# Two more output tiles between the last products of a projection, and a gate tile in front of a moment

## The chip, the cores and the metric

One NeuronCore of one Trainium2 chip runs the whole program. TensorE (PE in the profile, its weight loads PEld) multiplies 128 by 128 weight blocks with 128 x n operands and sums into banks of PSUM; VectorE (DVE), ScalarE (ACT) and GpSimd (POOL) do the rest; SyncE (SP) issues most of the DMAs. The metric is the device time of the program in microseconds, less is better.

## The reference

One inference step of a backbone of two layers over 640 tokens (512 latent and 128 context tokens) of width 1024: layer 0 mixes tokens by attention, layer 1 by a linear recurrence; each is followed by a SwiGLU feed-forward, and each sub-layer adds its output, times a gate, to the residual stream after a modulated RMS norm. The change lies where layer 1's recurrence ends and its feed-forward begins:

```python
y = (hs_f + hs_b).astype(xm.dtype) * jax.nn.gelu(gate)
return y @ w_out, ...                       # the recurrent output's projection
...
lat = lat + g1_l[:, None, :] * o_l          # residual, the same for ctx
f_l = _swiglu(_modulate(lat, norm_g[i, 1], sh2_l, sc2_l), ffn_w_gu[i], ffn_w_down[i])
```

with

```python
def _rms_norm(x, g):
    xf = x.astype(jnp.float32)
    y = xf * lax.rsqrt(jnp.mean(xf * xf, axis=-1, keepdims=True) + RMS_EPS)
def _swiglu(x, w_gu, w_down):
    gate, up = jnp.split(x @ w_gu, 2, axis=-1)
    return (jax.nn.silu(gate) * up) @ w_down
```

## The kernel before

**Layout.** Features lie on partitions, tokens along the free dimension. A width of 1024 is KT = 8 blocks of 128, and the 640 tokens are two halves CH of HT = 320. A float32 product is made of three: every operand is split into a high part (rounded to fp32r) and a low part (what is left), and a tile, one block of 128 outputs over one half of the tokens, sums high x high, high x low and low x high over the eight input blocks k: 24 matmuls. `chunk` and `some` (L235 to L237) write this for the projections, `plain` (L1189 to L1191) for the first feed-forward tiles.

**Weights.** `unit` loads a weight block (L169) into one of three `raw` buffers, makes its high part with ScalarE (L182, a cast) or, with `cast=True`, by a second load from DRAM on POOL's DMA queue that casts on the way (L180), and its low part with VectorE (L184). Slot "m" uses `whi`, `wlo`, slot "x" `whx`, `wlx`, three buffers each; the first `whx` of every three has a place of its own. `after` names an instruction of VectorE behind which the low part is put.

**Order.** The program is traced in the order of the code; a scheduler of the framework then sets the order of each engine's instructions by its own estimate of when each is ready, the earlier in the code first. An engine runs them in that order. `pin` (`issue_after`) is the only thing by which the code sets an order: the instructions in it come behind a named one of the same engine.

**PSUM.** Eight banks: one `at` for the sums of squares, three `mm`, three `mx`, one `mc`. `ps(tag)` takes a bank of a tag. `pg()` counts its calls and gives `mx` where the count modulo 5 is 1 or 3, else `mm`; `pg(False)` counts too, and always gives `mm`. The spread of a moment has no tag of its own in this phase and takes `mx`.

**`project_halves` (L1043).** It multiplies the recurrence's output y by its projection. Output blocks are f = 0 to 7. Five tiles begin early (both halves of 0 and 1, the first half of 2) with the input blocks k that are there; `turn` (L1054) then adds the last blocks k = 5, 6, 7 to all of them as VectorE delivers y (L1058 with y's high part, L1060 with its low part). y's last block comes in two halves of tokens, so `turn(KT - 1, ...)` is done for the tiles of the first half and then for those of the second. Block 3's first half stands between and around these (L1075): its weights' low part is pinned behind `ended`, VectorE's last step of the recurrence, and the last third of its products comes after the second `turn`. Blocks 4 to 7, first half, follow, then the first half's statistics, and then blocks 2 to 7 of the second half.

Each finished tile goes through `out`: VectorE adds it to x times the gate (L605), `square` makes ScalarE square the new x (L539, L542) and VectorE add the square to `ssq` (L544, block 7 excepted, whose square the matmuls take themselves), and SP stores x (L1046). `stat` is `moment` and `spread`: TensorE sums `ssq` over partitions (L558, L561), VectorE makes the variance (L563), POOL the power -1/2 (L565), VectorE a diagonal (L567), and TensorE spreads it over the partitions (L575). ScalarE copies the result (L1089), and `normed` (L1009 on VectorE, L1010 on ScalarE) and `halve` (L1422, L1424) make the normalised tokens and their high and low parts, the blocks B11 and B21 of the first half (`first_half`), B12 and B22 of the second (`second_half`).

**The feed-forward.** Of its 22 pairs of gate and up blocks, the first three (PLAIN) are six ordinary tiles for each half of the tokens: gate, up, gate, up, gate, up. `ffn_halves` loads all six weights, the low parts of the second and third pair pinned behind the last `ssq` addition (`self.sq`), and calls `plain` for the first half. `held` (L1122) keeps the second tile, the first up, behind the moment (at k = 0), and its blocks from k = 5 and the later tiles behind the spread, so that its first five blocks lie over the chain between the two. The gate tiles end in a Silu (L1197), the up tiles in a product (L1151). Then the second half's tokens are normalised, `plain` runs for them, `sums` and `sum_weights` form differences of tokens and of weights (POOL, L1033 and L1110) for the other 19 pairs, which use a scheme of seven products in place of eight, and the projection down is woven in between.

Of the kernel before, what the change touches and what calls it, by code (L numbers as in the profile page):

```python
# [12 lines left out]
ALU = mybir.AluOpType  # L13
# [4 lines left out]
KT = D // P  # L18
# [4 lines left out]
CH = ((0, 320), (320, 640))  # L23
# [6 lines left out]
NF = FF // P  # L30
# [12 lines left out]
HT = NTOK // 2  # L43
HB = KH * HT
DEH = 6
PLAIN = 3
# [77 lines left out]
def _pieces(t0, t1):  # L124
    return [(s, max(a, t0), min(b, t1)) for s, a, b in ((0, 0, NLAT), (1, NLAT, NTOK)) if max(a, t0) < min(b, t1)]


class _Step:
# [473 lines left out]
    def residual(self, f, t0, t1, ps, G, sq):  # L602
        for s, a, b in _pieces(t0, t1):
            xs = self.x[:, f, a:b]
            self.nc.vector.scalar_tensor_tensor(xs, ps[:, a - t0:b - t0], G[:, s, f:f + 1], xs, ALU.mult, ALU.add)  # L605
        if sq:
            self.square(f, t0, t1)

# [431 lines left out]
        self.halve("T4", k, self.x[:, k + KH, 0:HT])  # L1040
        self.nc.sync.dma_start(self.x[:, k + KH], xd[(k + KH) * P:(k + KH) * P + P])

    def project_halves(self, w, hi, lo, gk, key, xd, ended):  # L1043
        def out(f, t0, t1, ps):
            self.residual(f, t0, t1, ps, G, True)
            self.nc.sync.dma_start(xd[f * P:f * P + P, t0:t1], self.x[:, f, t0:t1])  # L1046
        G = self.need(self.gcols, gk)
        us = [self.unit(w[f], "mmx"[f], cast=f == 2) for f in range(3)]
        early = [(f, t0, t1) for f in range(3) for c, (t0, t1) in enumerate(CH) if c == 0 or f < KT - DEH]
        pss = [(self.ps("mx") if j % 2 else self.pg(False))[:, 0:HT] for j in range(len(early))]  # L1050
        for (f, t0, t1), ps in zip(early, pss):
            self.some(us[f], hi, lo, t0, t1, ps, range(KT - 3))

        def turn(k, turns, pin=None):  # L1054
            for (f, t0, t1), ps in turns:
                for part in us[f]:
                    with self.pin(pin):
                        pin = self.done = self.nc.tensor.matmul(ps, part[:, k], hi[:, k, t0:t1], start=False, stop=False).ins  # L1058
            for (f, t0, t1), ps in turns:
                self.done = self.nc.tensor.matmul(ps, us[f][0][:, k], lo[:, k, t0:t1], start=False, stop=(k == KT - 1)).ins  # L1060
                if k == KT - 1:
                    with self.pin(self.low):
                        out(f, t0, t1, ps)
        sides = [[e for e in zip(early, pss) if e[0][1:] == c] for c in CH]
        for k in range(KT - 3, KT - 1):
            turn(k, sides[0] + sides[1])
        us.append(self.unit(w[3], "m", ended, cast=True))
        turn(KT - 1, sides[0])
        t0, t1 = CH[0]
        ps = self.ps("mx")[:, 0:HT]  # L1070
        for j, (part, v) in enumerate(((0, hi), (0, lo), (1, hi))):
            if j == 2:
                turn(KT - 1, sides[1], self.done)
            for k in range(KT):
                self.done = self.nc.tensor.matmul(ps, us[3][part][:, k], v[:, k, t0:t1], start=(j == k == 0),  # L1075
                                                  stop=(j == 2 and k == KT - 1)).ins
        out(3, t0, t1, ps)
        for f in range(4, KT):
            us.append(self.unit(w[f], "xm"[f % 2]))
            out(f, *CH[0], self.chunk(us[f], hi, lo, *CH[0], pins={0: self.done} if f == 4 else {}))  # L1080
        self.rt = self.t([P, NTOK], F32, "r", 2)
        for c, (t0, t1) in enumerate(CH):
            for f in range(KT - DEH, KT) if c else ():
                out(f, t0, t1, self.chunk(us[f], hi, lo, t0, t1))
                j = f - KT + DEH
                for k in range(max(0, 2 * j - 2), 2 * j) if f < KT - 1 else ():
                    self.first_half(k, key)
            self.stat(t0, t1)
            self.nc.scalar.copy(self.rt[:, t0:t1], self.r[0][:, 0:t1 - t0])  # L1089

    def gate_weights(self, l, f):
# [89 lines left out]
    def plain(self, us, c, xd=None):  # L1181
        nc, n = self.nc, 0
        for j, pair in enumerate(us):
            for u, (hi, lo) in enumerate(pair):
                ps = self.pg()[:, 0:HT]
                for k in range(KT):
                    xh, xl = [self.X[f"B{1 + k // KH}{1 + c}{p}"][:, k % KH] for p in "hl"]
                    with self.held(n, k):
                        nc.tensor.matmul(ps, hi[:, k], xh, start=(k == 0), stop=False)  # L1189
                    nc.tensor.matmul(ps, hi[:, k], xl, start=False, stop=False)  # L1190
                    nc.tensor.matmul(ps, lo[:, k], xh, start=False, stop=(k == KT - 1))  # L1191
                n += 1
                if u:
                    self.hidden(j, c, ps, g)
                else:
                    g = self.t([P, HT], F32, "g", 3, self.sb)
                    nc.scalar.activation(g, ps, AF.Silu)  # L1197
            if c:
                self.sums(j, xd)

    def ffn_halves(self, l, key, xd):
        us = [[self.unit(self.i["gu"][l, c * NF + f], None, self.sq if f else None) for c in range(2)] for f in range(PLAIN)]
        self.hold = True
        self.plain(us, 0)
        self.hold = False
        self.wx, self.share = 0, False
        qs = [None] * PLAIN
        for k in range(KH):
            self.second_half(k, key)
        self.plain(us, 1, xd)  # L1210
        for k in range(KH - 1):
            self.last_sum(k, xd)

        def rest():
            self.sums(KH - 1, xd)
            self.last_sum(KH - 1, xd)
        f0 = 0
        for ci, n in enumerate(CHN):
            for j in range(n):
                f = f0 + j  # L1220
                if f < PLAIN:
                    continue
                if f == len(qs):
                    qs.append(self.gate_weights(l, f))
                    self.pair_a(qs[f])
                if j:
                    self.sum_weights(qs[f])
                    self.pair_c(qs[f - 1])
                    self.last_weights(qs[f])
                self.pair_b(qs[f], j)  # L1230
            if f >= PLAIN:
                self.pair_c(qs[f])
            w = self.i["dn"][l, :, :, f0:f0 + n]
            f0 += n
            if f0 == NF:
                self.share = True
                self.project_last(w, self.hhi, self.hlo, (l, 5))
            else:
                qs.append(self.gate_weights(l, f0))
                self.pair_a(qs[f0])  # L1240
                self.sum_weights(qs[f0])
                self.last_weights(qs[f0])
                self.project_part(w, self.hhi, self.hlo, (l, 5), rest if f0 == PLAIN else None)
# [57 lines left out]
    def turn(self, table, step):  # L1301
        if table != self.table:
            self.table = table
            with self.pin(self.last_act):
                self.last_act = self.nc.scalar.preload_act_table(table).ins
        with self.pin(self.last_act):
            self.last_act = step().ins
# [139 lines left out]
    def run(self):  # L1447
        nc, tc, i, o = self.nc, self.tc, self.i, self.o
# [68 lines left out]
        xd = dram.tile([D, NTOK], F32, tag="xd", name="xd")  # L1517
# [11 lines left out]
        yhi = self.big()  # L1529
        ylo = self.big()  # L1530
        wp = self.ctx.enter_context(tc.tile_pool(name="wp", bufs=1, reuse_waits="tile"))
        with self.phase("lru", at=1) as lp:
            A, B, C, G = {}, {}, {}, {}
# [14 lines left out]
            for t in range(KT + 2):  # L1548
# [7 lines left out]
                if t > KT:  # L1556
                    ended = self.lru_end(t - 2, *B.pop(t - 2), G.pop(t - 2), yhi, ylo)
# [11 lines left out]
        with self.phase("ffn1", at=1, mx=3, mc=1, wx=2) as fp:  # L1569
            self.X = {}  # L1570
            self.blocks(x1, ("B11h", "B11l", "B21h", "B21l"))
            self.blocks(x2, ("B22h", "B22l", "T1h", "T1l"))
            self.blocks(self.t([P, 2 * KH, HT], F32R, "xt", 1, fp), ("T4h", "T4l"))
            self.X["B12h"], self.X["B12l"] = self.X["T4h"], self.X["T4l"]
            self.project_halves(i["wlo"], yhi, ylo, (1, 2), (1, 1), xd, ended)
            nc.gpsimd.dma_start(o["nh"], self.st)
            self.hhi, self.hlo = self.big(n=PITCH), self.big(n=PITCH)
            for t, n in ((self.hhi, "T2"), (self.hlo, "T3")):
                self.blocks(t, (n + "h", n + "l"))
            self.hhi, self.hlo = [t[:, :, 0:NTOK] for t in (self.hhi, self.hlo)]  # L1580
            self.ffn_halves(1, (1, 1), xd)
# [19 lines left out]
```

## Time and profile before

| | us |
|---|---|
| median of 3 runs | 1512.21 (1511.01 to 1512.85) |
| profiled execution | 1510.6 |
| its span, first to last instruction | 1508.8 |
| TensorE busy | 1482.4 |
| VectorE busy | 1061.8 |
| ScalarE busy | 698.1 |
| `project_halves` on TensorE, from about | 985 to 1063 |

A row of the timeline has a start, a duration, engine, line, operation, output and inputs, the count, and in brackets the idle time of the engine just before it with what ended it. A row of a window has its stretch and length, busy time and instructions of PE, PEld, DVE, ACT and POOL, the granted TensorE clock (1.00 is full), the DMA engines' busy share and GB/s. The waits list engine, line, what it waited for, total, times and the longest. Matmuls overlap: one of 320 columns is shown as 0.31 us long, while the next starts 0.15 us after it.

### The profile page before, as it was taken

To read this page: it belongs to the slowest core of one execution; us is meant where nothing else is said; L and a number is where in the kernel's file an instruction comes from. 1 tells how busy PE (TensorE), PEld (TensorE's weight loads), DVE (VectorE), ACT (ScalarE), POOL (GpSimd) and SP (SyncE) were. 2 spreads that over 40 slices of the span, in tenths; PEclk is the share of its full clock that TensorE was granted. 3 is DMA by queue.
4 is the path that set the end of the run, shared out by engine and by line. 5 is a ranking of instruction groups with operands and counts; after the bars stand their busy time and mean duration, and the time that the engine had idled before them with its cause. 6 is when DMAs were issued, how large, how long until landed. Compare 5 with 4: busy or idle time off the path is not lost. (4 is left out here: it accounts for less than half of the span.)

```text
span 1508.8 us, 26147 instructions
## 1 busy us (share of the span) xinstructions
PE 1482.4 (98%) x10389; PEld 1434.3 (95%) x10389; DVE 1061.8 (70%) x2017; ACT 698.1 (46%) x1267; POOL 229.3 (15%) x264
## 2 busy tenths in 40 slices
PE   9999999999999999999999999999999999999997
PEld 6999999899999999999999988889999999999997
DVE  5778998679989997434443768986875665665555
ACT  4676766664332123312321569875534342524243
POOL 0112232101111110000000000000431323232211
PEclk9999999999999999999999999999999999999999
DMA  9655765446556664222222444334243131313221
GB/s 376 175 145 159 189 187 172 118 152 184 184 179 205 203 201 141 62 85 84 65 76 84 156 135 123 119 127 171 77 134 95 59 113 56 112 57 101 67 57 70
DMA packets 72905, 198.34 MB, mean 131 GB/s; under 512 B 8112, under 2 KB 24656, under 8 KB 72656
## 3 DMA queue, kind: packets, MB, share of 16 engines
q1 hardware_dynamic: 57392, 142.32, 29.8%
q0 software_dynamic: 14816, 53.69, 11.9%
q8 instruction: 81, 1.33, 0.4%
q10 hardware_dynamic: 576, 0.68, 0.1%
q14 instruction: 40, 0.33, 0.1%
HBM read 180.53 MB, written 8.92 MB: 126 GB/s over the span
## 5 line engine op out<-in xcount | busy, mean ns | idle before, releaser
L236 PE MATMUL mm<-big,whi 128*128 128x320 f32 (+3 forms) x1215 | 377.6, 311 | 1.0 <-DVE big L1424 0.7
L235 PE MATMUL mm<-big,whi 128*128 128x320 f32 (+3 forms) x1215 | 375.6, 311 | 2.9 <-DVE x L605 1.4
L237 PE MATMUL mm<-big,wlo 128*128 128x320 f32 (+3 forms) x1215 | 375.2, 310 | 0.0
L235 PEld LDWEIGHTS mm<-big,whi 128*128 128x128 f32 x1215 | 228.0, 188 | 5.3 <-issue 1.6
L236 PEld LDWEIGHTS mm<-big,whi 128*128 128x128 f32 x1215 | 228.4, 188 | 3.1 <-DVE big L1424 1.3
L237 PEld LDWEIGHTS mm<-big,wlo 128*128 128x128 f32 x1215 | 228.7, 188 | 1.1
L264 DVE SCALAR_TENSOR_TENSOR mprod<-mraw,csb 128x1024 f32<-128x1024 f32 x160 | 195.1, 1219 | 12.1 <-DMA mraw<-in_wm 11.6
L605 DVE SCALAR_TENSOR_TENSOR x<-mm,G,x 128x128 f32<-128x128 f32 (+2 forms) x193 | 77.8, 434 | 78.1 <-PE mm L237 78.1
L182 ACT CAST whi<-raw 128x1024 fp32r<-128x1024 f32 (+1 forms) x70 | 72.8, 1040 | 112.4 <-PE mm L236 64.3
L184 DVE TENSOR_TENSOR wlo<-raw,whi 128x1024 fp32r<-128x1024 f32 (+1 forms) x87 | 105.7, 1215 | 22.9 <-ACT whi L182 10.1
L236 PE MATMUL mm<-big,whx 128*128 128x320 f32 (+3 forms) x357 | 110.9, 311 | 0.0
L237 PE MATMUL mm<-big,wlx 128*128 128x320 f32 (+3 forms) x357 | 110.5, 310 | 0.0
L235 PE MATMUL mm<-big,whx 128*128 128x320 f32 (+3 forms) x357 | 110.2, 309 | 0.0
L260 POOL DMA_DIRECT2D mraw<-in_wm x80 | 42.9, 537 | 352.7 <-DVE mprod L264 254.0
L236 PE MATMUL mx<-big,whi 128*128 128x320 f32 (+3 forms) x285 | 88.1, 309 | 0.0
L235 PE MATMUL mx<-big,whi 128*128 128x320 f32 (+3 forms) x285 | 88.0, 309 | 0.0
L237 PE MATMUL mx<-big,wlo 128*128 128x320 f32 (+3 forms) x285 | 87.9, 308 | 0.0
L182 ACT CAST whx<-raw 128x1024 fp32r<-128x1024 f32 (+1 forms) x39 | 40.1, 1028 | 85.8 <-PE mm L236 48.2
L236 PE MATMUL mx<-big,whx 128*128 128x320 f32 (+3 forms) x248 | 76.8, 310 | 0.0
L237 PE MATMUL mx<-big,wlx 128*128 128x320 f32 (+3 forms) x248 | 76.8, 310 | 0.0
L235 PE MATMUL mx<-big,whx 128*128 128x320 f32 (+3 forms) x248 | 76.5, 308 | 0.0
L1422 ACT CAST whi<-raw 128x1024 fp32r<-128x1024 f32 (+1 forms) x41 | 41.3, 1007 | 72.0 <-PE mm L236 44.5
(388 smaller groups left out, 3721.3 us busy)
## 6 DMA issues: line engine op xcount, KB each, us to landing
raw<-in_gu SPq DMA_DIRECT2D x88, 512.0 KB, 3.5
mraw<-in_wm POOLq DMA_DIRECT2D x80, 512.0 KB, 4.0
raw<-in_dn SPq DMA_DIRECT2D x24, 512.0 KB, 3.7
sw<-in_wm SPq DMA_DIRECT2D x16, 512.0 KB, 10.9
raw<-in_wqk SPq DMA_DIRECT2D x16, 512.0 KB, 4.8
raw<-in_wi SPq DMA_DIRECT2D x16, 512.0 KB, 3.5
whi<-in_wi POOLq DMA_DIRECT2D x16, 512.0 KB, 3.8
raw<-in_dn SPq DMA_DIRECT2D x16, 448.0 KB, 3.3
```

The costliest lines, as they stand in the source:

```text
L182: nc.scalar.copy(hi, raw)
L184: self.low = nc.vector.tensor_tensor(lo, raw, hi.bitcast(F32), ALU.subtract).ins
L235: nc.tensor.matmul(ps, hi[:, k], xhi[:, k, s], start=(k == 0), stop=False)
L236: nc.tensor.matmul(ps, hi[:, k], xlo[:, k, s], start=False, stop=False)
L237: self.done = nc.tensor.matmul(ps, lo[:, k], xhi[:, k, s], start=False, stop=(k == last)).ins
L260: nc.gpsimd.dma_start(w, self.i["wm"][l * 6 + j - 2, f])
L264: nc.vector.scalar_tensor_tensor(prod, w, 1.0, self.csb[:, s], ALU.mult, ALU.mult, accum_out=out[:, s, f:f + 1])
L605: self.nc.vector.scalar_tensor_tensor(xs, ps[:, a - t0:b - t0], G[:, s, f:f + 1], xs, ALU.mult, ALU.add)
L1422: self.nc.scalar.copy(hi, v)
```

## The change

`project_halves`: blocks 3 and 4 are both loaded before the last `turn`s, both with `cast=True`, block 4's low part pinned behind block 3's. The first half of block 4 gets the bank `mc`. Their products are chained by pins in a fixed order: first `turn`, two thirds of block 3, second `turn`, two thirds of block 4, the last third of 3, the last third of 4. Block 5's low part is pinned behind the residual of block 2's first half, and its first half takes an `mm` bank by name; 6 and 7 go on with `pg()`.

`ffn_open` starts the generator into which `plain` is turned. It is called when the last tile of the second half is out: the first pair's weights are loaded (the up's low part now also pinned behind `self.sq`), the first gate tile is traced, then the moment, then the first five blocks of the up tile, then the spread, pinned behind those. The rest follows as before.

```diff
@@ residual
-            self.nc.vector.scalar_tensor_tensor(xs, ...)
+            self.added = self.nc.vector.scalar_tensor_tensor(xs, ...).ins
@@ project_halves
-        us.append(self.unit(w[3], "m", ended, cast=True))
+        for f in (3, 4):
+            us.append(self.unit(w[f], "xm"[f % 2], ended, cast=True))
+            ended = self.low
+        t0, t1 = CH[0]
+        more = {f: self.ps(v)[:, 0:HT] for f, v in ((3, "mx"), (4, "mc"))}
+
+        def part(f, pieces):
+            for p, v in pieces:
+                for k in range(KT):
+                    with self.pin(self.done):
+                        self.done = self.nc.tensor.matmul(more[f], us[f][p][:, k], v[:, k, t0:t1], start=(v is hi and p == k == 0),
+                                                          stop=(p == 1 and k == KT - 1)).ins
         turn(KT - 1, sides[0])
-        t0, t1 = CH[0]
-        ps = self.ps("mx")[:, 0:HT]
-        for j, (part, v) in enumerate(((0, hi), (0, lo), (1, hi))):
-            if j == 2:
-                turn(KT - 1, sides[1], self.done)
-            for k in range(KT):
-                self.done = self.nc.tensor.matmul(ps, us[3][part][:, k], v[:, k, t0:t1], start=(j == k == 0),
-                                                  stop=(j == 2 and k == KT - 1)).ins
-        out(3, t0, t1, ps)
-        for f in range(4, KT):
+        added = self.added
+        part(3, ((0, hi), (0, lo)))
+        turn(KT - 1, sides[1], self.done)
+        part(4, ((0, hi), (0, lo)))
+        for f in (3, 4):
+            part(f, ((1, hi),))
+            out(f, t0, t1, more[f])
+        us.append(self.unit(w[5], "m", added))
+        more[5] = self.pg(False)[:, 0:HT]
+        part(5, ((0, hi), (0, lo), (1, hi)))
+        out(5, t0, t1, more[5])
+        for f in range(6, KT):
             us.append(self.unit(w[f], "xm"[f % 2]))
-            out(f, *CH[0], self.chunk(us[f], hi, lo, *CH[0], pins={0: self.done} if f == 4 else {}))
+            out(f, t0, t1, self.chunk(us[f], hi, lo, t0, t1))
...
-            self.stat(t0, t1)
+            if c:
+                first = opening()
+                next(first)
+                moment = self.moment(t0, t1)
+                next(first)
+                with self.pin(self.done):
+                    self.spread(moment)
+            else:
+                self.stat(t0, t1)
@@ plain
+                    if self.hold and n == 1 and k == 5:
+                        yield
                     with self.held(n, k):
-                        nc.tensor.matmul(ps, hi[:, k], xh, start=(k == 0), stop=False)
+                        self.done = nc.tensor.matmul(ps, hi[:, k], xh, start=(k == 0), stop=False).ins
...
+                yield
@@ ffn_open, ffn_halves
+    def ffn_open(self, l):
+        self.us = [[self.unit(self.i["gu"][l, c * NF], None, self.sq if c else None) for c in range(2)]]
+        self.first = self.plain(self.us, 0)
+        self.hold = True
+        return self.first
+
     def ffn_halves(self, l, key, xd):
-        us = [[self.unit(self.i["gu"][l, c * NF + f], None, self.sq if f else None) for c in range(2)] for f in range(PLAIN)]
-        self.hold = True
-        self.plain(us, 0)
+        us, gu = self.us, self.i["gu"]
+        us += [[self.unit(gu[l, c * NF + f], None, self.sq) for c in range(2)] for f in range(1, PLAIN)]
+        for _ in self.first:
+            pass
```

More of the change, by code (lines that the diff above doesn't have):

```diff
@@ L604, in residual @@
             xs = self.x[:, f, a:b]
-            self.nc.vector.scalar_tensor_tensor(xs, ps[:, a - t0:b - t0], G[:, s, f:f + 1], xs, ALU.mult, ALU.add)
+            self.added = self.nc.vector.scalar_tensor_tensor(xs, ps[:, a - t0:b - t0], G[:, s, f:f + 1], xs, ALU.mult, ALU.add).ins
         if sq:
@@ L1041, in last_sum, with project_halves @@
         self.nc.sync.dma_start(self.x[:, k + KH], xd[(k + KH) * P:(k + KH) * P + P])
-    def project_halves(self, w, hi, lo, gk, key, xd, ended):
+    def project_halves(self, w, hi, lo, gk, key, xd, ended, opening):
         def out(f, t0, t1, ps):
@@ L1209, in ffn_halves @@
             self.second_half(k, key)
-        self.plain(us, 1, xd)
+        for _ in self.plain(us, 1, xd):
+            pass
         for k in range(KH - 1):
@@ L1574, in run @@
             self.X["B12h"], self.X["B12l"] = self.X["T4h"], self.X["T4l"]
-            self.project_halves(i["wlo"], yhi, ylo, (1, 2), (1, 1), xd, ended)
+            self.project_halves(i["wlo"], yhi, ylo, (1, 2), (1, 1), xd, ended, lambda: self.ffn_open(1))
             nc.gpsimd.dma_start(o["nh"], self.st)
```

## The prediction, made before the changed kernel was run

> **Names.** f3a is output tile 3 over tokens 0 to 319, f3b over tokens 320 to 639, so too for f0 to f7. g0, u0, g1, u1, g2, u2 are the six feed-forward tiles over the first tokens in program order; u0 is the one that L1188 holds behind the moment and the spread. A tile is 24 matmuls.
>
> **What bounds the kernel now.** I read the page first, then TensorE's waits, then its stretches by window around L1043.
>
> ```profile
> span 1508.8 us, 26147 instructions
> PE 1482.4 (98%) x10389; PEld 1434.3 (95%) x10389; DVE 1061.8 (70%) x2017; ACT 698.1 (46%) x1267; POOL 229.3 (15%) x264
> ```
>
> ```profile
> PE at L558 <- DVE ssq L544: 4.5, 2, 3.8
> ```
>
> ```profile
> 1006.20:1015.40 9.20, 6.47 (x41) 5.65 (x40) 8.50 (x17) 3.02 (x5) 0.55 (x1) 1.00 0.40 143
> 1015.40:1052.60 37.20, 37.18 (x258) 37.12 (x258) 23.18 (x49) 17.90 (x35) 0.87 (x1) 1.00 0.56 197
> 1052.60:1056.60 4.00, 0.19 (x2) 0.03 (x1) 3.32 (x9) 2.96 (x7) 0.00 (x0) 1.00 0.22 82
> 1057.60:1061.00 3.40, 3.40 (x16) 3.40 (x15) 2.37 (x4) 0.00 (x0) 0.85 (x1) 0.50 0.69 205
> ```
>
> TensorE is busy 98% of the span, so only its holes are worth anything, and the longest in the whole trace, 3.8 us, is the one before the last moment (L558). The windows give PE, PEld, DVE, ACT and POOL busy time, then the clock. The stage of the change has two holes, 1006 to 1015 (2.7 us idle) and 1052.6 to 1056.6 (3.8 us), with none between. After the second the clock stands at 0.50 for 3.4 us.
>
> **The first hole: f3a and f4a between the last products.**
>
> ```profile
> 1006.22 1.18 PE L1075 MATMUL mx<-big,whi 128*128 128x320 f32 x7
> 1008.18 0.41 PE L1058 MATMUL mm<-big,whi 128*128 128x320 f32 x1 [0.78 <-ACT big L1398]
> ...
> 1012.60 1.44 PE L1075 MATMUL mx<-big,wlo 128*128 128x320 f32 x8 [0.59 <-DVE wlo L184]
> 1015.42 0.38 PE L235 MATMUL mm<-big,whi 128*128 128x320 f32 x1 [1.38 <-DVE x L605]
> ```
>
> ```profile
> 1014.73 1.00 DVE L605 SCALAR_TENSOR_TENSOR x<-mm,G,x 128x320 f32<-128x320 f32 x2
> ```
>
> Removed: the waits of 0.59 and 1.38 us. With f4a's 16 high products in front of f3a's low ones, f3's low part is long there, and f4a takes the bank mc, so nothing waits for a first residual's buffer. Lost: the first row's seven matmuls, which now fill part of the wait for the last y, are chained behind the first last products; TensorE idles from about 1006.4 to 1008.18, 1.8 us. From there 87 matmuls (9 and 6 last products, 72 for f3a, f4a, f5a) at the 0.147 us by which such rows follow each other take 12.8 us: f5a ends at 1021.0. Now, 1022.52 (row below) is where three such tiles are done: 1.5 us gained. f5's low part, pinned behind f2a's residual, may be late by up to 0.7 us: four subtractions and residuals stand ahead of it on VectorE, from the 1014.73 of the residual row. So 1021.0 to 1021.7.
>
> But what follows is f6a, whose weights come late:
>
> ```profile
> 1012.74 1.31 SPq L169 DMA_DIRECT2D raw<-in_wlo  x2
> ```
>
> ```profile
> 1020.64 1.05 ACT L182 CAST whx<-raw 128x1024 fp32r<-128x1024 f32 x1 [1.33 <-DMA raw<-in_wlo]
> 1022.44 1.05 ACT L182 CAST whi<-raw 128x1024 fp32r<-128x1024 f32 x1 [0.75 <-DMA raw<-in_wlo]
> ```
>
> ```profile
> 1023.19 1.22 DVE L184 TENSOR_TENSOR wlx<-raw,whx 128x1024 fp32r<-128x1024 f32 x1
> ```
>
> ```profile
> 1022.52 0.31 PE L235 MATMUL mm<-big,whx 128*128 128x320 f32 x1
> ```
>
> ```profile
> 1043.16 0.83 PE L575 MATMUL mx<-dg,ones 128*128 128x128 f32 x6
> 1043.75 0.39 PE L235 MATMUL mx<-big,whi 128*128 128x320 f32 x1
> ```
>
> The two loads of f6 and f7 leave when f3's and f4's raw buffers are free (1012.74), and ScalarE waits for their data until 1020.64 and 1022.44. f6a's low part is there at 1020.64 + 1.05 + 1.22 = 1022.9 at the earliest, f7's high part at 1023.5. Today f2b fills that gap. It cannot any more, and here I read the order of buffers out of the last two rows: f3b, in bank tag mx, starts right behind the spread of the first moment, which writes mx too, though f4b and f5b (mm) ran long before it. So one tag's buffers are given out in program order. With f4a and f3a outside the pool the count of `pg` falls by one, and the tags become f6a, f7a mm; f2b mx; f3b mm; f4b mx; f5b, f6b mm; f7b mx; g0 mm; u0 mx. f2b, f4b and f7b now queue behind that spread; f3b queues behind f7a. TensorE thus idles from 1021.0 or 1021.7 to 1022.9 or 1023.6. Two matmuls of f6a fit before it, so the eight tiles that now start at 1022.52 in effect start at 1022.6 to 1023.3. I take **+0.5 us**. Then f6a, f7a, f3b, f5b and f6b, 17.6 us, cover the first moment's chain: f7a ends near 1030.3 instead of 1033.5, and the spread moves up as far, so those behind it find their buffers. The end of f7b, now 1052.63, becomes 1053.1.
>
> One more transfer is added: f4's high part comes by POOL's DMA instead of ScalarE's cast (ScalarE saves 1.05 us).
>
> ```profile
> 1005.00:1010.00 5.00, 4.22 (x29) 3.96 (x28) 4.79 (x11) 0.46 (x1) 0.00 (x0) 1.00 0.00 0
> 1015.00:1020.00 5.00, 4.58 (x31) 4.61 (x32) 4.90 (x13) 2.82 (x6) 0.00 (x0) 1.00 1.03 408
> ```
>
> Behind f3's cast it falls where the DMA engines stand idle (share 0.00) and costs nothing. If it left only after 1010, it would meet x and the two loads at share 1.03: 512 KB at 408 GB/s, 1.3 us, the upper bound. I take 0. [...]
>
> **The second hole: g0 ahead of the last moment.**
>
> ```profile
> 1052.48 0.31 PE L237 MATMUL mm<-big,wlo 128*128 128x320 f32 x1
> 1056.60 0.46 PE L558 MATMUL at<-ones,ssq 128*128 128x128 f32 x2 [3.81 <-DVE ssq L544]
> ...
> 1058.26 0.61 PE L1189 MATMUL mm<-big,whi 128*128 128x320 f32 x1
> ...
> 1061.78 0.83 PE L575 MATMUL mx<-dg,ones 128*128 128x128 f32 x6
> 1062.37 0.39 PE L1189 MATMUL mx<-big,whx 128*128 128x320 f32 x1
> ...
> 1067.29 0.31 PE L1189 MATMUL mm<-big,whx 128*128 128x320 f32 x1
> ```
>
> ```profile
> 1059.78 0.15 DVE L563 TENSOR_SCALAR var<-at 128x3 f32<-128x3 f32 x1
> 1060.96 0.56 DVE L567 TENSOR_TENSOR dg<-ident,rs 128x384 f32<-128x384 f32 x1 [1.03 <-POOL rs L565]
> ```
>
> Now, from 1052.63 to g1 at 1067.29, 14.66 us: 3.97 empty, moment 1.66, u0's first 15 matmuls 3.52, spread 0.59, g0 3.60, u0's last nine 1.32. g0 (mx) comes behind the spread by the same buffer order; in the new program it has mm, allocated before the moment, and can go first. Its 24 matmuls take 3.52 us, and the last sum and the square of f7b end meanwhile: f4b, the last tile before f7b in the new order, ends 3.5 us before it, which leaves time for the sums. So the empty 3.97 goes. The moment takes 1.4 us and u0's 15 matmuls 2.2 us at full clock. From the moment's end to the spread the rows show 1059.78 to 1061.78, 2.0 us, plus the wait for VectorE, now 1.2 us with three weight subtractions queued ahead; so 2.0 to 3.2 us, and TensorE waits 0 to 1.0 us. After: 3.5 + 1.4 + 2.2 + 0.5 + 0.6 + 1.3 = 9.5 us, **-5.1 us**.
>
> [...]
>
> **What is late next.** The spread itself comes only about 1 us earlier, TensorE 4.6 us. So the second tokens' inputs, which hang on the spread, lose slack:
>
> ```profile
> 1074.75 1.70 DVE L1424 TENSOR_TENSOR big<-x,big 128x320 fp32r<-128x320 f32 x4
> ```
>
> ```profile
> 1081.37 0.31 PE L1189 MATMUL mm<-xt,whx 128*128 128x320 f32 x1
> ```
>
> ```profile
> 1092.87 0.41 PE L1189 MATMUL mm<-xt,whi 128*128 128x320 f32 x1 [0.77 <-ACT g L1197]
> ```
>
> ```profile
> 1064.75 0.63 ACT L1422 CAST wuh<-raw 128x512 fp32r<-128x512 f32 x1 [1.67 <-DMA raw<-in_gu]
> ```
>
> ```profile
> 1091.43 1.05 ACT L1422 CAST whx<-sum 128x1024 fp32r<-128x1024 f32 x1 [3.71 <-POOL sum L1110]
> 1092.38 0.43 ACT L1197 ACTIVATE g<-mm 128x320 f32<-128x320 f32 x1
> ```
>
> The last of these inputs (1074.75 to 1076.45) are wanted 1.8 us after 1081.37, by then 1078.6: still over 2 us early. The Silu at 1092.38 is the tight place; I allow 0.5 us, between nothing and the 3.6 us of the first rival below. Sum: +0.5 - 5.1 + 0.5 = **-4.1 us** on the profiled execution's 1510.6 (span 1508.8 and 1.8 around it), 1506.5. The median of the runs is 1512.21, 1.6 above, so I forecast 1508.1 us.
>
> Costed at nothing: u0's low part, now pinned behind the last sum, is the first subtraction there and ends under the moment. The shifted pool counter also swaps banks in the last projection; five head tiles fit as before, so 0, within 0.5 either way.
>
> **Rivals.**
> - *The Silu row takes it back.* ScalarE runs in order: the Silu that frees the next bank stands behind a cast that waits 3.71 us for POOL. POOL's chain hangs on the spread. If the order stays, the tile at 1092.87 starts only 1.0 to 1.7 us earlier, however early TensorE is. For it: the row already stops TensorE by 0.77. Against: g0's 3.5 us move from behind the spread to before it, so the Silu is due before that cast and should be put first. Time 1510.8. Chance 0.19.
> - *g0 does not go first.* Nothing pins the moment behind g0; if g0's low part (its buffer is free only after f2b) is late, the order stays. Then only the earlier sums help, some 1.5 us, against +0.5: 1511.2. Chance 0.12.
> - *Slower: the raw buffers.* u0's low part used to be made early; now it waits for the last sum and holds its raw buffer, so g2's load leaves after it, and the load behind g2, whose cast stands at 1064.75 ahead of ScalarE's normalising of the second tokens, comes a load, a cast and a subtraction later (3.5 + 1.05 + 1.22 us). If the last sum ends near 1053 this lands at 1065, no loss; if it stays near 1056.4, 3 to 4 us later, and with the Silu order unchanged the tile at 1092.87 starts that much late: 1515. It decides from 1 us of lateness. Chance 0.12.
>
> **How the numbers follow.** Forecast 0.57: its own range is -6.1 (loads 1 us earlier, no waits) to -2.4: 1506.1 to 1509.8. With the first two rivals 0.88 is covered, so 1505.8 to 1512.5. 0.2% is 3.0 us, about what a measurement of this kernel tells from no change: faster 0.56, same 0.31, slower 0.13.
>
> **What would show it.** Right: no idle before L558 over 0.5 us, L1189 rows ahead of L558, no clock row at 0.50, a hole of some 2 us before f6a with f2b behind L575, g1 about 4.6 us earlier. Wrong: L558 ahead of g0; f2b ahead of L575 (the buffer order misread, 1 us better); a hole before f6a of over 3 us; a wait at the Silu row over 2 us.

## The result and the profile after

The changed kernel takes 1506.62 us (median of 11 runs, 1504.91 to 1508.83) beside 1511.54 for the kernel before (11 runs, 1509.77 to 1512.87): a ratio of 0.9968, 95% interval 0.9958 to 0.9977, or 4.9 us less (3.5 to 6.3). The forecast was 1508.1.

The profiled execution took 1506.85 us; its page begins:

```profile
span 1505.1 us, 26144 instructions
PE 1482.0 (98%) x10389; PEld 1434.7 (95%) x10389; DVE 1063.6 (71%) x2017; ACT 698.1 (46%) x1266; POOL 225.1 (15%) x265
```

TensorE's busy time is the same (1482.4 before); the span is 3.7 us shorter. What went is idle time, but part of it comes back elsewhere. TensorE's waits from 985 us on, with total, number of times and longest:

```profile
PE mm L1058 <- ACT big L1430: 1.8, 1, 1.8
...
PE mm L235 <- ACT whx L182: 1.1, 1, 1.1
PE mm L237 <- DVE wlx L184: 0.7, 1, 0.7
...
PE mm L1212 <- DVE g L1172: 0.3, 1, 0.3
```

The wait of 3.8 us ahead of L558 is not among them, nor those of 0.59 and 1.38. The waits of 1.1 and 0.7 us ahead of f6a are new, and the wait for y's last block (L1058) has grown from 0.8 to 1.8. The same stretch in TensorE's timeline:

```profile
1008.94 0.42 PE L1058 MATMUL mm<-big,whi 128*128 128x320 f32 x1 [1.82 <-ACT big L1430]
...
1020.55 1.32 PE L1077 MATMUL mm<-big,wlo 128*128 128x320 f32 x8
1022.99 0.41 PE L235 MATMUL mm<-big,whx 128*128 128x320 f32 x1 [1.13 <-ACT whx L182]
1023.24 0.31 PE L236 MATMUL mm<-big,whx 128*128 128x320 f32 x1
1024.25 0.42 PE L237 MATMUL mm<-big,wlx 128*128 128x320 f32 x1 [0.70 <-DVE wlx L184]
...
1042.60 0.83 PE L575 MATMUL mx<-dg,ones 128*128 128x128 f32 x6
1043.18 0.39 PE L235 MATMUL mx<-big,whx 128*128 128x320 f32 x1
...
1055.73 0.31 PE L1212 MATMUL mm<-big,whx 128*128 128x320 f32 x1
...
1059.24 0.38 PE L558 MATMUL at<-ones,ssq 128*128 128x128 f32 x2
...
1062.81 0.91 PE L575 MATMUL mx<-dg,ones 128*128 128x128 f32 x6
...
1064.87 0.31 PE L1212 MATMUL mm<-big,whx 128*128 128x320 f32 x1
...
1100.63 0.31 PE L1153 MATMUL mx<-big,whi 128*128 128x320 f32 x1
```

L1212 is the `plain` line that was L1189, L1153 the product line that was L1132. The rows show that f6a waits twice behind the end of f5a (1022.99, 1024.25), that f2b and f4b stand behind the first spread (1042.60, 1043.18), that g0 begins at 1055.73, right behind f7b and ahead of the moment, which waits for nothing, and that g1 begins at 1064.87.

The two traces begin differently in their first microseconds, so where two kernels are compared, times are **aligned** from here on at the first product with y's last block, 1008.18 before and 1008.94 after: 0.76 is taken off each later time of the changed kernel. The rows shown stay as their trace has them. f7b then ends at 1054.97 (before: 1052.63), g1 begins at 1064.11 (1067.29), the first product behind the six second-half tiles at 1099.87 (1103.53).

So the head of the change (all that stands ahead of f7b's end) loses 2.3 us in this execution, and the tail (from there to g1) gains 5.5. The loss is larger than the forecast's 0.5, and the windows show what came on top of the two holes (length, busy PE, PEld, DVE, ACT, POOL, clock, DMA share, GB/s):

```profile
1021.80:1025.40 3.60, 1.77 (x11) 1.45 (x11) 2.43 (x5) 2.95 (x5) 0.00 (x0) 1.00 0.97 353
1025.40:1028.90 3.50, 3.50 (x16) 3.50 (x15) 2.55 (x5) 0.72 (x2) 0.00 (x0) 0.51 1.05 408
...
1055.70:1059.20 3.50, 3.50 (x26) 3.50 (x25) 3.17 (x6) 1.97 (x3) 0.00 (x0) 1.00 0.14 49
```

Behind the holes the clock stands at 0.51 for 3.5 us: 16 products there instead of the 26 of the last row. Before the change it stood at full speed there, and at 0.50 behind the hole at L558 instead.

### The profile page after: what moved, and what is told of

Read it like the earlier page. It is cut to its first block, busy times and chain, and to the rows that moved or that the text cites. A ratio compares the mean times of both kernels' runs of the same rounds, so it can differ in the third digit from the quotient of the medians.

```text
span 1505.1 us, 26144 instructions
## 1 busy us (share of the span) xinstructions
PE 1482.0 (98%) x10389; PEld 1434.7 (95%) x10389; DVE 1063.6 (71%) x2017; ACT 698.1 (46%) x1266; POOL 225.1 (15%) x265
## 5 line engine op out<-in xcount | busy, mean ns | idle before, releaser
L605 DVE SCALAR_TENSOR_TENSOR x<-mm,G,x 128x320 f32<-128x320 f32 (+2 forms) x192 | 77.6, 436 | 80.3 <-PE mm L237 79.0
L235 PE MATMUL mm<-big,whx 128*128 128x320 f32 (+3 forms) x349 | 108.7, 312 | 1.1 <-ACT whx L182 1.1
L236 PE MATMUL mm<-big,whx 128*128 128x320 f32 (+3 forms) x349 | 109.3, 313 | 0.0
L235 PE MATMUL mx<-big,whi 128*128 128x320 f32 (+3 forms) x277 | 85.7, 309 | 0.4 <-ACT big L1454 0.4
L236 PE MATMUL mx<-big,whi 128*128 128x320 f32 (+3 forms) x277 | 85.8, 310 | 0.0
```

Of the source, the lines that this page charges most:

```text
L235: nc.tensor.matmul(ps, hi[:, k], xhi[:, k, s], start=(k == 0), stop=False)
L236: nc.tensor.matmul(ps, hi[:, k], xlo[:, k, s], start=False, stop=False)
L605: self.added = self.nc.vector.scalar_tensor_tensor(xs, ps[:, a - t0:b - t0], G[:, s, f:f + 1], xs, ALU.mult, ALU.add).ins
```

## The experiments

All kernels ran beside the kernel before on the same chip. The table gives the ratio to it, and from one profiled execution each, aligned as above, the difference from the profile of the kernel before (in us, less is earlier) at five places: f7b's end, the second spread, g1's first product, the first product behind the second-half tiles, and the span's end.

| kernel | ratio (95%) | f7b ends | spread | g1 | product | end |
|---|---|---|---|---|---|---|
| changed | 0.9968 (0.9958 to 0.9977) | +2.34 | +0.27 | -3.18 | -3.66 | -4.4 |
| changed again | 0.9973 (0.9961 to 0.9984) | +0.68 | -1.38 | -4.83 | -5.37 | -6.3 |
| head only | 1.0002 (0.9994 to 1.0011) | +2.81 | +0.93 | +0.94 | +1.29 | +0.8 |
| head, banks shifted | 0.9994 (0.9986 to 1.0003) | +2.62 | +0.67 | -0.58 | -1.02 | +0.5 |
| tail only | 0.9975 (0.9963 to 0.9987) | 0.0 | -0.47 | -3.91 | -4.66 | -5.0 |
| tail only again | 0.9973 (0.9962 to 0.9984) | 0.0 | -0.49 | -3.93 | -4.98 | -5.7 |
| g0's bank only | 0.9982 (0.9973 to 0.9990) | 0.0 | -0.15 | -3.59 | -2.85 | -3.3 |
| hole filled | 0.9965 (0.9952 to 0.9979) | +1.16 | -0.91 | -4.36 | -4.39 | -4.7 |
| f2b early | 0.9954 (0.9941 to 0.9966) | -1.58 | -2.64 | -6.09 | -6.68 | -7.5 |
| f2b early, f3a free | 0.9948 (0.9935 to 0.9960) | -2.29 | -3.35 | -6.79 | -7.52 | -7.6 |
| tail, low parts later | 0.9977 (0.9967 to 0.9986) | 0.0 | -1.96 | -5.47 | -4.99 | -5.1 |
| all together | 0.9957 (0.9944 to 0.9970) | -2.22 | -4.32 | -7.84 | -6.45 | -7.5 |

### The head alone

The projection's part of the change alone, and the bank counter put back ahead of the feed-forward, so that g0 takes `mx` and u0 `mm` as before:

```diff
@@ ffn_halves, as it was before the change
         self.hold = True
+        self.ng += 1
         self.plain(us, 0)
```

> Head part of the change alone; the bank counter is put back before the feed-forward, so the first gate tile g0 keeps a bank of tag mx and stays behind the second spread, as before the change. Theory (the head is a loss): in the changed kernel's trace the hole before the last products of y is 1.82 us, two holes stand before f6a (1.13 and 0.70 us), and 3.4 us of half clock follow; together f7b ended 2.3 us later than before. So +2.3 us against before (1513.9), or +0.7 (1512.2) if the half clock does not come here; the hole ahead of L558 stays at 3.5 to 4 us. Rival (the head gains what it removes, the waits of 0.59 and 1.38 us, as was its working up to f5a): -1.5 us, 1510.0.

Its waits from 1000 to 1100 us:

```profile
PE at L558 <- DVE ssq L544: 1.9, 1, 1.9
PE mm L1058 <- ACT big L1412: 1.7, 1, 1.7
PE mm L235 <- ACT whx L182: 1.6, 1, 1.6
...
PE mm L237 <- DVE wlx L184: 0.7, 1, 0.7
```

Its windows behind the two holes, at f6a and at L558:

```profile
1024.00:1027.40 3.40, 3.40 (x13) 3.40 (x14) 3.14 (x6) 0.92 (x3) 0.00 (x0) 0.50 1.02 397
...
1058.10:1061.50 3.40, 3.40 (x17) 3.40 (x16) 2.79 (x4) 0.00 (x0) 0.47 (x1) 0.51 0.50 152
```

The rival falls: the head gains nothing by itself. f7b ends 2.8 us later, near the theory's +2.3. But the whole is not 2.3 us slower: its ratio of 1.0002 lies between 0.9 us faster and 1.7 slower. Where did the loss go? The wait ahead of L558 is 1.9 us instead of 3.8. Most of the lateness was swallowed by this hole, in which TensorE waits for VectorE's last sum, and 0.9 us was left at the spread. The expected 3.5 to 4 us at L558 was wrong, and with it the expected time.

### The head with its shift of banks

The same without that line: g0 takes `mm`, u0 `mx`, and the feed-forward's code stands where it stood before.

```diff
@@ against the head alone
-        self.ng += 1
```

> Head part of the change alone, with the shift of the bank counter that it brings (g0 gets a bank of tag mm, u0 one of tag mx), the feed-forward's code where it was before. Theory (tags decide what may run ahead of a spread): g0 runs ahead of L558 though its code stands behind it; u0 in turn falls wholly behind the spread, so 2 to 3 us stand empty between moment and spread. Against the head alone -2.5 to -3.5 us, so about 1510.5 in all (-1.0 against before). Rival (the order of the code decides, the generator was needed): as the head alone, 1513.9 or 1512.2.

Its waits:

```profile
PE mx L575 <- DVE dg L567: 2.2, 1, 2.2
...
PE mm L235 <- ACT whx L182: 1.4, 1, 1.4
PE mm L237 <- DVE wlx L184: 0.7, 1, 0.7
```

g0's first product, right behind f7b:

```profile
1056.49 0.30 PE L1202 MATMUL mm<-big,whx 128*128 128x320 f32 x1
```

There is no wait at L558 any more, and one of 2.2 us ahead of the spread: g0 went ahead of the moment with no change to its place in the code, and u0 fell behind the spread, whose tag it now shares. By the ratio the kernel is 0.9 us faster than before (interval 2.1 faster to 0.5 slower), where 1.0 was expected; the head alone on the same chip was 0.3 slower. The step between the two is thus 1.2 us, where 2.5 to 3.5 was expected, and their intervals overlap; in the traces it is 1.5 at g1.

### The tail alone

`ffn_open`, the generator and the pinned spread, with `project_halves` as before up to there. Against the kernel before:

```diff
-            self.stat(t0, t1)
+            if c:
+                first = opening()
+                next(first)
+                moment = self.moment(t0, t1)
+                next(first)
+                with self.pin(self.done):
+                    self.spread(moment)
+            else:
+                self.stat(t0, t1)
...
```

> Tail part of the change alone (gate tile, moment, five blocks of the up tile, spread), the projection's head as before. Theory (the tail makes the whole gain and the head takes part of it back): f7b ends where it did, 1052.6 in the span, and 9.1 us instead of 14.7 stand between there and g1: -5.5 us, 1506.0, at or a little below the changed kernel. Rival (both parts gain): -2.5 to -3.5 us only, 1508.5, above the changed kernel by 2 us.

This kernel is 3.8 us faster by the ratio (2.0 to 5.6), and 5.0 at the trace's end. The interval holds the theory's 5.5 as well as the rival's 2.5 to 3.5; the trace speaks for the theory that the tail makes the gain, though not for all of its 5.5. f7b ends where it did, and the gain lies between there and g1 (-3.91) and in the second-half tiles. TensorE's row at the spread:

```profile
1061.69 0.91 PE L575 MATMUL mx<-dg,ones 128*128 128x128 f32 x6 [1.35 <-DVE dg L567]
```

and VectorE's rows ahead of it in the same kernel:

```profile
1055.40 1.08 DVE L544 TENSOR_TENSOR ssq<-ssq,sq 128x320 f32<-128x320 f32 x2
1056.40 1.22 DVE L184 TENSOR_TENSOR wlo<-raw,whi 128x1024 fp32r<-128x1024 f32 x1
1057.54 1.22 DVE L184 TENSOR_TENSOR wlx<-raw,whx 128x1024 fp32r<-128x1024 f32 x1
1058.67 1.22 DVE L184 TENSOR_TENSOR wlo<-raw,whi 128x1024 fp32r<-128x1024 f32 x1
1059.81 0.15 DVE L563 TENSOR_SCALAR var<-at 128x3 f32<-128x3 f32 x1
1060.99 0.56 DVE L567 TENSOR_TENSOR dg<-ident,rs 128x384 f32<-128x384 f32 x1 [1.03 <-POOL rs L565]
```

Here is the next bound: three low parts stand between the last sum and the variance, and TensorE waits 1.35 us for the diagonal behind them. The same three stand there in the changed kernel, with no gap between the last sum's end (1057.60) and the variance (1060.92), so there too the spread goes by the moment at which VectorE is done with the last sum.

### g0's bank alone

The kernel before, one expression changed, no generator:

```diff
-                ps = self.pg()[:, 0:HT]
+                ps = self.pg(not self.hold or n > 0)[:, 0:HT]
```

> Before, with one expression changed: the first gate tile g0 takes a bank of tag mm, the code in its old order, no generator. Theory (what held g0 back was only its bank, given out behind that of the spread): g0 runs ahead of L558 and u0's first 15 products stay between moment and spread, so the same 5.5 us as with the tail alone, 1506.0. Rival (the place in the code held it back): nothing moves, 1511.5.

Its timeline at the moment:

```profile
1052.53 0.31 PE L1189 MATMUL mm<-big,whx 128*128 128x320 f32 x1
...
1056.50 0.46 PE L558 MATMUL at<-ones,ssq 128*128 128x128 f32 x2 [0.30 <-DVE ssq L544]
```

g0 (L1189, bank `mm`) begins right behind f7b: what held it back was its bank, given out behind the spread's, not its place in the code. At g1 the lead is 3.59, 0.3 less than with the tail alone. Then less arrives: the ratio is 0.9982, a gain of 2.7 us (1.5 to 4.1) instead of the 5.5 expected. Its waits show where it is lost:

```profile
PE mm L1189 <- DVE g L1151: 1.5, 1, 1.5
```

TensorE waits 1.5 us for the bank of a second-half tile. The tail alone, with its other sequence of banks and loads, does not have this wait; which of the two keeps it away was not tested.

### The hole ahead of f6a filled

Twelve idle multiplications in the changed kernel (the trace shows each as two rows of 128 columns, so 24):

```diff
         out(5, t0, t1, more[5])
+        self.keep(self.ps(), 12)
```

> The changed kernel with 12 idle multiplications of 128 columns put on TensorE between f5a and f6a, where it waits 1.13 us for the high part of f6's weights. In the changed kernel's trace 3.41 us of half clock begin 1.2 us after those holes; the head alone and the head with the shift showed it too, the tail alone and the bank of g0 alone, which have no holes there, did not. Theory A (the idle time just before brings the half clock): with about 0.7 us of it filled, no half clock between 1020 and 1035, f7b ends 1.7 us earlier than in the changed kernel (aligned at the arrival of y's last block: 1053.3 instead of 1055.0). Theory B (it comes from something else, as the load of DMA and the other engines there): it stays, and f7b ends at 1055.0. For the whole time theory C says that the wait behind the moment decides: the spread then comes at most 0.4 us earlier, since three subtractions of weights (1.14 us apart) stand ahead of the variance on VectorE, so 0 to -0.7 us against the changed kernel, that is 1505.2 to 1506.6 beside a before of 1511.0; were f7b's end what counts, -1.7.

The fill in its timeline, and the windows over and behind it:

```profile
1021.34 2.84 PE L218 MATMUL at<-ident,ones 128*128 128x128 f32 x24
```

```profile
1021.00:1024.40 3.40, 3.40 (x31) 3.40 (x30) 1.95 (x3) 2.81 (x4) 0.00 (x0) 1.00 0.98 331
1024.40:1027.90 3.50, 3.50 (x26) 3.50 (x25) 2.90 (x6) 0.97 (x3) 0.00 (x0) 1.00 1.08 410
```

These windows are full, at clock 1.00, with the DMA engines as busy as in the changed kernel (0.98 and 1.08). That fits theory A, not theory B, but it is one profile, and the next experiment shows the unfilled kernel without a half clock too: so it isn't shown that the fill is what kept it away. f7b ends 1.2 us earlier than in the changed kernel's first profile (1.7 expected; the fill's row takes 2.84 us where the two holes had been 1.83). The time, 0.9965, cannot be told from the changed kernel's, as theory C had it.

### The changed kernel and the tail alone again, on one chip

> The changed kernel once more, as it is, beside the tail alone and a last version on one chip. The half clock behind the two holes ahead of f6a: if it hangs on the holes, it stands there again (1024 to 1030 in the span); if on the moment at which a window of the clock happens to begin, it may be missing. Time: 0.9968 of before, as on record, 1506.5 beside a before of 1511.4.

> The tail part alone once more, to stand beside the changed kernel on one chip. If the head is worth nothing in the whole, within 1.0 us of the changed kernel on either side; if the head gains 1.5 us there, 1.5 us above it.

The changed kernel's second profile has the same two holes and **no** half clock. In rows (timeline, then the windows behind the holes):

```profile
1022.48 0.41 PE L235 MATMUL mm<-big,whx 128*128 128x320 f32 x1 [0.98 <-ACT whx L182]
...
1023.74 0.42 PE L237 MATMUL mm<-big,wlx 128*128 128x320 f32 x1 [0.70 <-DVE wlx L184]
```

```profile
1021.40:1025.00 3.60, 1.92 (x11) 1.56 (x11) 2.54 (x5) 3.23 (x5) 0.00 (x0) 1.00 1.01 368
1025.00:1028.40 3.40, 3.40 (x26) 3.40 (x25) 2.80 (x5) 0.52 (x2) 0.00 (x0) 1.00 1.05 391
```

f7b ends at +0.68 instead of +2.34, 1.66 us less. Of this 0.1 is there already at f6a's last wait, so the half clock itself costs about 1.55 us, and all of it is still there at the first product (-5.37 against -3.66). The same program has it in one execution and not in the other, under the same load of the DMA engines (1.01 and 1.05), which speaks against theory B above.

By time, the two kernels are the same: 0.9973 and 0.9973, 1506.95 and 1506.84 us. **The head is worth nothing that can be measured; the tail makes the gain.**

The two profiles, neither with a half clock, show what the head trades. With it f7b ends 0.7 us later, and yet the spread comes 0.9 us earlier (-1.38 against -0.49): VectorE's last sum ends 1.9 us behind f7b (1055.54 behind 1053.67) instead of 3.5 (1055.21 behind 1051.74). At the span's end 0.6 us of this is left, too little for the times to show.

### f2b ahead of f6a

The holes removed by work that is ready: the second half of block 2 traced between f5a and f6a.

```diff
         out(5, t0, t1, more[5])
+        out(2, *CH[1], self.chunk(us[2], hi, lo, *CH[1]))
         for f in range(6, KT):
...
-            for f in range(KT - DEH, KT) if c else ():
+            for f in range(3, KT) if c else ():
```

> The changed kernel with the second half of block 2 (f2b) traced between f5a and f6a, so that it stands ahead of the first spread again and lies over the loads of f6 and f7. Theory: the holes of 1.13 and 0.70 us and the half clock (1.7 us) go; f7b ends at about 1051.3 (aligned), 3.5 us earlier than in the changed kernel and 1.3 earlier than before the change. The whole time gains less, for the moment's chain is bound by VectorE: the spread comes 1.5 to 2.5 us earlier than in the changed kernel, so about -2 us, 1504.0 to 1505.0 beside a before of 1511.0. Rival 1 (f7b's end counts alone): -3.5, 1502.6. Rival 2 (the chain doesn't move at all): 0, 1506.1.

```profile
PE mm L1058 <- ACT big L1431: 1.8, 1, 1.8
...
PE mx L575 <- DVE dg L567: 0.9, 1, 0.9
```

Both holes and the half clock are gone; f7b ends 1.58 us earlier than before, as the theory had it (1.3). The end gains less than f7b did: from the changed kernel's second profile, which has no half clock either, f7b moves by 2.26 us and the spread by 1.26, since a wait of 0.9 us for VectorE's diagonal stands there again. The ratio is 0.9954, 1504.4 us beside 1511.4, as the theory had it; its interval (0.9941 to 0.9966) overlaps with the changed kernel's, so the times alone don't show the step.

### f3a's first products free

In that kernel, the first seven products of f3a without their pin:

```diff
-                    with self.pin(self.done):
+                    with self.pin(None if f == 3 and p == 0 and v is hi and k < KT - 1 else self.done):
```

> As the kernel before it in this call, and the first seven products of f3a are not chained, so that they may run while TensorE waits 1.8 us for y's last block, as they did before the change. Theory: the hole shrinks to 0.8 us and everything up to f7b comes 1.0 us earlier (1050.3 aligned); the end gains 0 to 1.0 us against that kernel, by how far VectorE's queue holds the spread: 1503.5 to 1504.5 beside a before of 1511.0. Rival (f5a's weights or the low parts are late in their turn): no gain up to f7b.

```profile
PE mm L1058 <- ACT big L1431: 0.8, 1, 0.8
```

The wait for y's last block is 0.8 us instead of 1.8, and f7b comes 0.71 us earlier (1.0 expected). With a ratio of 0.9948 this is by its median the best version of the study, 7.9 us under the kernel before (6.0 to 9.8); its interval touches that of the changed kernel only at the edge (0.9960 against 0.9958 and 0.9961), and overlaps widely with that of the kernel without the step. In the trace nearly all of the step is lost behind the second-half tiles: -7.52 at the first product and -7.6 at the end, where the kernel without it has -6.68 and -7.5.

### The low parts behind the diagonal

In the tail alone, and then in the version just shown, the low parts of the second and third pair pinned behind L567 instead of the last sum:

```diff
-        us += [[self.unit(gu[l, c * NF + f], None, self.sq) for c in range(2)] for f in range(1, PLAIN)]
+        us += [[self.unit(gu[l, c * NF + f], None, self.dg) for c in range(2)] for f in range(1, PLAIN)]
```

> The tail part alone, with the low parts of the second and third pair of feed-forward weights pinned behind the moment's diagonal (L567) instead of behind the last sum: on VectorE one subtraction instead of three stands ahead of the variance. Theory (in the tail alone those three set the spread: the moment's products are over at about 1058.2 aligned to its own row, the variance starts at 1059.8): variance, diagonal and spread 1.2 to 1.5 us earlier, the wait of 1.35 us ahead of the spread goes, -1.3 us against the tail alone, 1505.7 beside a before of 1511.0 (the tail alone: 0.9975 of it, 1507.2). Rival (the low parts that come later are late for g1 and u1, a wait at g1 takes the place): no gain or up to 1 us slower.

> All that the runs pointed to together: the changed kernel, f2b traced ahead of f6a, the first seven products of f3a unchained, and the low parts of the second and third pair of feed-forward weights behind the moment's diagonal. Its forerunner without the last step stood at 0.9948 and still waits 0.88 us ahead of the second spread for VectorE. Theory (a gain at the spread is given back where the tail alone with the same step gave it back, at the Silu that frees the bank of the second tokens' tiles, 1.26 us): within 0.7 us of its forerunner, 1502.8 to 1504.2 beside a before of 1511.4. Rival (with 2 us more of head start that Silu is not what TensorE waits for): -0.9 us or more, 1502.5.

VectorE in the tail alone with this step:

```profile
1056.51 1.23 DVE L184 TENSOR_TENSOR wlo<-raw,whi 128x1024 fp32r<-128x1024 f32 x1
1058.29 0.16 DVE L563 TENSOR_SCALAR var<-at 128x3 f32<-128x3 f32 x1 [0.56 <-PE at L561]
```

The three low parts did set the spread: with one, the variance waits for the moment itself, and the spread comes 1.5 us earlier. But the gain does not reach the end. ScalarE in the same kernel:

```profile
1092.21 1.05 ACT L1441 CAST whx<-sum 128x1024 fp32r<-128x1024 f32 x1 [7.70 <-POOL sum L1118]
...
1094.90 0.43 ACT L1207 ACTIVATE g<-mm 128x320 f32<-128x320 f32 x1
```

```profile
1095.39 0.41 PE L1199 MATMUL mm<-xt,whi 128*128 128x320 f32 x1 [1.26 <-ACT g L1207]
```

ScalarE waits 7.70 us for POOL's sum of weights, and the Silu that frees the next bank stands four instructions behind. TensorE waits 1.26 us for it; with all steps together 2.16. That is what the prediction feared, a Silu behind a cast that waits for POOL, one gate tile later than there, and it does take back what arrives too early: the ratios are 0.9977 and 0.9957, no better than without the step (0.9975 and 0.9948). For the tail alone that is the rival's result, though the wait that takes the gain is at the second tokens' tiles and not at g1. For all steps together the place is the theory's, and 0.9957 of 1511.4, 1504.9, lies a little above its 1502.8 to 1504.2.

## Why the prediction was right, and where it was not

The direction, the mechanism of the tail and the range were right: 4.9 us less by the median, 4.1 forecast. That the two lie so close is partly luck, as the terms show. Step by step:

- **The first hole's waits**: right. There are 1.82 us ahead of the last products (1.8 forecast), and the waits of 0.59 and 1.38 are gone. The added transfer costs nothing, as argued: the DMA engines stand idle again from 1005.8 to 1010.8 (share 0.00).
- **The hole ahead of f6a and f2b behind the spread**: right. Without the half clock f7b ends 0.68 us late; +0.5 was forecast. The order of banks was read rightly from two rows, and the kernel with g0's bank alone shows it as a cause, for g0.
- **The clock behind the holes**: wrong, and this is the step that failed. The sum counts no loss of clock behind the holes ahead of f6a, and the moment and u0's 15 matmuls at full clock. No run shows that holes of such a length always leave the clock at full; it was the author's estimate. In this stage the profile before has one half clock, behind the hole of 3.81 us, and none behind those of 0.78, 0.59 and 1.38 (clock 1.00 from 1006.20 to 1052.60). In the changed kernel the moment and u0 did run at 1.00 (1059.20 to 1064.80), but behind holes of 1.13 and 0.70 us the profiled execution has 3.41 us of half clock, about 1.55 us that the sum did not have; the second profile of the same program has none. The sign "no clock row at 0.50" failed with it in the first profile, and so did "g1 about 4.6 us earlier" (3.2; 4.8 in the second). In the profile before, 2.43 of the 3.81 us lie in the 3.413 us ahead of the half clock and 1.38 in front of these.
- **The second hole**: right in mechanism, a little small. f7b's end to g1 is 9.14 us in the first and 9.15 in the second profile instead of 14.66: -5.5, forecast -5.1. About 1.6 of it is the half clock behind L558 in the profile of the kernel before (moment and u0's first 15 matmuls take 3.6 us instead of 5.2); whether each of its timed runs has that is not known.
- **What is late next**: the sign was wrong. From g1 to the first product it is 35.76 us instead of 36.24, -0.5 where +0.5 was allowed. The order at the Silu came as argued, as ScalarE's rows in the changed kernel show:

```profile
1083.21 0.43 ACT L1220 ACTIVATE g<-mm 128x320 f32<-128x320 f32 x1
1083.65 0.46 ACT L1454 CAST big<-g 128x320 fp32r<-128x320 f32 x1
1089.60 1.05 ACT L1454 CAST whx<-sum 128x1024 fp32r<-128x1024 f32 x1 [5.49 <-POOL sum L1131]
```

  The Silu is in front of the cast that waits for POOL, and the tile that waited 0.77 us for it starts without a wait. The 0.3 us in the list of waits stand one tile later and are ended by VectorE's product (L1172).
- **The rivals.** "The Silu row takes it back" did not happen in the changed kernel, but its mechanism shows, one gate tile later, in the two kernels with the low parts later, whose spread comes another 1.0 to 1.5 us earlier. "g0 does not go first" is refuted by its row at 1055.73. The slower one, by the raw buffers, left no sign: u0's low part is the first behind the last sum, and no wait of TensorE's for weights follows.

So the terms were +0.7 (+2.3 with the half clock), -5.5 and -0.5: -5.4 or -3.7 up to the first product, and 0.8 to 0.9 us more after it, of which 0.4 is two waits near 1235 us (0.20 and 0.50 before) that became one of 0.26. The forecast lay near the median partly because a term too dear (+0.5 for -0.5) stood against one not seen.

What stays open: how often the half clock comes at this place in the timed runs, and whether the head is worth some tenths without it; its interval of about 1.7 us to either side does not tell. Each timed run's mean clock is on record. The profiles with no half clock ahead of the program's end have a mean of 0.998 or 0.999, the one with one such stretch 0.998, those with two 0.996. Of the changed kernel's 18 runs two stand at 0.999, eight at 0.998 and eight at 0.995 to 0.997: so such stretches are common, but the mean does not say where they lie.

## What to carry to other kernels

Where an instruction may go is decided by its buffer as well as by its place in the code: g0, whose bank was given out behind the waiting spread's, did not pass the spread, and changing the tag alone gave 2.7 of the 4.9 us. A gain in front of a wait for another engine was swallowed there in part (f2b: 2.26 us at f7b's end, 1.26 at the spread), and so was a loss (the head alone: 2.81 and 0.93); ask what that engine has queued, here three subtractions of 1.22 us ahead of the variance. Filling a hole with work that is ready (f2b) moved f7b by 2.3 us and the end of the trace by 1.2.

## What the hardware showed beyond what was expected

In each of four traces the half clocks lie whole multiples of 3.4133 us apart, and the length of one hole does not decide whether one follows. The stretches at 0.5 in their clock records (start in us of the span; the last of each belongs to the program's end):

```
before                 1057.58                    1504.73
changed          8.32  1025.49                    1499.94
head only              1024.01   1058.14          1505.29
head, shifted   25.09  1025.20                    1506.48
```

All but the last of each row last 3.413 us, and their distances are whole multiples of 3.4133: 1017.17 is 298.0 of them, 34.13 is 10.0, 1000.11 is 293.0, 447.15 is 131.0. What sets this distance is not shown.

In the 3.413 us ahead of a half clock from 1000 us on TensorE is idle for 2.43 (before), 1.61 (changed), 2.27 and 1.89 (head only) and 2.09 us (head, shifted); ahead of 8.32 in the changed kernel it is idle for 1.87. The hole of 1.82 us ahead of 1008.94 in the changed kernel had no half clock behind it; counted back from 1025.49 in five steps of 3.4133, 1008.42 cuts it in two (1.30 and 0.52). Nor did one follow holes of 0.98 and 0.70 us in the changed kernel's second profile, 1.52 with g0's bank only, 1.76 with the hole filled, 2.19 (head, shifted, ahead of the spread) or 2.16 with all steps together: the products behind these stand 0.15 us apart, where those in the half clock of the head alone are 0.27 apart. So idle time just ahead is not the whole rule, and a limit is not shown.
